# Moving the input projection's elementwise work from GpSimd to VectorE and ScalarE

## The chip, the cores and the metric

The kernel runs on one core of a Trainium2 chip. Its time is device time in microseconds of one execution, given as the median of several runs. The core has five instruction streams that run at once and wait for each other by semaphores: TensorE (PE, matrix multiplication into the accumulator memory PSUM), VectorE (DVE), ScalarE (ACT, functions and scaled copies), GpSimd (POOL, here used for elementwise operations) and SyncE (SP), which only issues DMA transfers. Each stream runs its instructions strictly in the order in which they were written out: an instruction that waits holds up everything behind it on the same engine.

## The reference

One layer of a bidirectional encoder, 1024 tokens of width 1024, float32. Cut to what the change touches, the first sub-layer is:

```
h = rms_norm(x); proj = h @ w_in
aq, ak, av, dqkv, dgate, dalpha, dbeta = split(proj)
aq, ak = rope(aq), rope(ak)                      # x1*cos - x2*sin, x2*cos + x1*sin
attn = window_attention(aq, ak, av, sink)        # +-128 tokens
q, k, v = silu(conv5(dqkv)); q, k = l2norm(q), l2norm(k)
g = -exp(a_log) * softplus(dalpha + dt_bias); beta = sigmoid(dbeta)
# gated delta rule in chunks, once forwards and once backwards:
decay[i, j] = exp(sum of g between j and i)
lower = strict_triangle((k*beta) @ k.T * decay); u, w = solve(I + lower, ...)
qk = (q @ k.T) * decay (triangle);  state recurrence over the chunks
mix = concat(attn, delta) @ w_out
```

Cross-attention and a feed-forward layer follow; the change does not touch them.

## The kernel before, in words

Matrix products that must keep float32 accuracy are made of three products in the reduced format F32R: each operand is split into a high part `hi` (a rounded copy, ScalarE, L102) and a low part `lo` (the difference, L103), and hi*hi, lo*hi and hi*lo are added in PSUM (`gemm_b`, L259). `load_w` loads a weight tile (`wraw`), splits it into `whi` and `wlo`, and takes the engine for the low part as an argument; there are two buffers of each.

The input projection has 22 column blocks of 128. For each of four heads the delta part takes three of them (`delta_proj`), convolves them (`conv`: two copies out of PSUM and a first tap on ScalarE, L281 and L282, then four taps on VectorE, L284, then Silu on ScalarE, L285) and prepares the chunk matrices (`prep`). `prep(h)` works on two halves of four chunks of 128 tokens, interleaved. For a half it builds `gm`, for each direction the triangle mask times the head's log decay `G` (L459, POOL), and multiplies it with a triangle in float32 on TensorE (L460); `E` is the exponential of the sum (L462). The products k*k (`U`) and q*k (`pc`) are multiplied by `E` on VectorE, and `pc` is masked twice into `pm` (L496, POOL), one for each direction, which are stored through DRAM for the later scan.

`base_inverse(g)` inverts the 32 x 32 diagonal blocks of two heads: thirty pairs of short VectorE operations (L536 `tmpb`, L538 `A`), each waiting for the one before. `levels(h)` builds the 128 x 128 inverse from them: block-diagonal tiles D5, D6, Z0 and Z1 are made by a mask (L579, half of them on POOL), with small matmuls (L595, L601) between. `attn_proj` applies the rotary embedding: VectorE makes `sn` (L737) and `rop` (L738), four DMAs move `sn`'s quarters to other partitions (`rot`, L742), and `rop + rot` is formed on POOL (L743) and stored. `window` is one block of window attention; `scan` is the recurrence, which begins when the levels are stored.

Python code lists the stages in the tables ORDER_1 (`D`: projection of a head, `P`: prep, `B`: base inverse), ORDER_2 (`L`: levels, `A`, `V`, `G`: attention, value and gate projections, `W`: two windows) and ORDER_3 (the scan). A scheduler then sets the order of each engine's instructions from priorities and its own estimates of their lengths, so a moved instruction also moves others.

Of the kernel before, what the change touches and what calls it, by code (L numbers as in the profile page):

```python
# [10 lines left out]
F32 = mybir.dt.float32  # L11
# [8 lines left out]
P = 128  # L20
# [3 lines left out]
NT = S // P  # L24
# [51 lines left out]
def tile_hybrid_block(  # L76
# [16 lines left out]
    def f32(ap):  # L93
        return ap.bitcast(F32)

    def bc(ap, axis, shape):
        return ap.unsqueeze(axis).to_broadcast(list(shape))
# [39 lines left out]
    sm = p12.enter_context(pool("sm", 1))  # L137
    C0, C1 = _AT["mUi"], _AT["mU"]
    C = sm.tile([P, C1 - C0], F32, name="C")
    mU_s = sm.tile([P, P], F32, name="mU_s")  # L140
    mL_s = sm.tile([P, P], F32, name="mL_s")
    prm = sm.tile([P, 24], F32, name="prm")
    nega = sm.tile([P, 8], F32, name="nega")
    p1 = ExitStack()
# [97 lines left out]
    nc.scalar.copy(cols, pt[:, :P])  # L242
    nc.sync.dma_start(CE, consts[:, C1:])
    nc.sync.dma_start(C, consts[:, C0:C1])
    nc.vector.tensor_copy(mU_s, cm["mU"])
    nc.vector.tensor_copy(mL_s, cm["mL"])

    nc.sync.dma_start(prm[:, 0:8], a_log[0].rearrange("d h -> (d h)").partition_broadcast(P))
    nc.sync.dma_start(prm[:, 8:16], dt_bias[0].rearrange("d h -> (d h)").partition_broadcast(P))
# [12 lines left out]
    def proj(src_cols, eng=None):  # L262
        whi, wlo = load_w(src_cols, KT, P, eng)
        pp = [pg.tile([P, 512], F32, tag="pg", name="pg") for _ in range(2)]
        gemm_b(whi, wlo, hT, pp)
        return pp
# [82 lines left out]
    dump("G", G)  # L349
    dump("beta", beta)  # L350


    pt = small()
    pv = pt[:, 0:192].rearrange("p (s d n) -> p s d n", s=3, d=2)
# [85 lines left out]
    def prep(h, kc, qc, vc):  # L440

        g, hh = h // 2, h % 2
        for src, i in ((kc, 2), (qc, 3)):
            nc.sync.dma_start(d_kv[g][:, :, hh, i].rearrange("c p n -> p c n"), src.rearrange("p (c n) -> p c n", c=NT))
        def part(b):
            c4 = slice(4 * b, 4 * b + 4)

            def turned(src):
                p_ = small()
                for j in range(4):  # L450
                    o = (4 * b + j) * P
                    nc.tensor.transpose(p_[:, j * P:(j + 1) * P], src[:, o:o + P], ident)
                return p_.rearrange("p (c n) -> p c n", c=4)


            pa = small()
            for d, (mi, ml) in enumerate((("mUi", mL_s), ("mLi", mU_s))):
                gm = t2.tile([P, 4, P], F32, tag="gm", name="gm")
                nc.gpsimd.tensor_tensor(gm, bc(G[:, d, h, c4], 2, (P, 4, P)), bc(cm[mi], 1, (P, 4, P)), ALU.mult)  # L459
                nc.tensor.matmul(pa, ml, gm.rearrange("p c n -> p (c n)"), start=(d == 0), stop=(d == 1))  # L460
            E = t2.tile([P, 4, P], F32, tag="E", name="E")
            nc.scalar.activation(E, pa.rearrange("p (c n) -> p c n", c=4), AF.Exp)  # L462

            def squares(pk, rev):
                ss = t2.tile([P, 4], F32, tag="ss4", name="ss4", bufs=4)
                for j in range(4):
                    jk = t2.tile([P, P], F32, tag="jk", name="jk")
                    o = 3 - j if rev else j
                    nc.scalar.activation(jk, pk[:, j, :], AF.Square, accum_out=ss[:, o:o + 1])
                return ss  # L470

            kv = t2.tile([P, 4, 2, P], F32, tag="kv", name="kv")
            yield
            pk = turned(kc)
            nc.scalar.copy(kv[:, :, 0, :], pk)
            ss = squares(pk, False)
            nc.gpsimd.tensor_scalar(xk[:, h, c4], ss, EPS, None, ALU.add)
            nc.gpsimd.tensor_tensor(rootk[:, h, c4], xk[:, h, c4], phalf[:, 0:4], ALU.pow)
            if hh and b:
                beta_rows(g)  # L480
            for i, src in ((2, kc), (3, qc)):
                yield
                p_ = small().rearrange("p (c n) -> p c n", c=4)
                for j in range(4):
                    o = (4 * b + j) * P
                    nc.tensor.matmul(p_[:, j, :], kc[:, o:o + P], src[:, o:o + P], start=True, stop=True)
                if i == 2:
                    U = t2.tile([P, 4, P], F32, tag="U", name="U")
                    nc.vector.tensor_tensor(U, p_, E, ALU.mult)
                    nc.sync.dma_start(d_u[g][hh, c4].rearrange("c p n -> p c n"), U)  # L490
                else:
                    pc = t2.tile([P, 4, P], F32, tag="pc", name="pc")
                    nc.vector.tensor_tensor(pc, p_, E, ALU.mult)
                    for d, mi in enumerate(("mUi", "mLi")):
                        pm = t2.tile([P, 4, P], F32, tag="pm", name="pm", bufs=3)
                        nc.gpsimd.tensor_tensor(pm, pc, bc(cm[mi], 1, (P, 4, P)), ALU.mult)  # L496
                        unsaved.append((d_pz[g][d][c4, :, hh, 0].rearrange("c p n -> p c n"), pm))
            yield

            nc.gpsimd.tensor_scalar(epsq[:, g, :, 1 - b, hh], squares(turned(qc), b == 0), P * EPS, P * EPS * EPS,  # L500
                                    ALU.mult, ALU.add)
            yield
            nc.vector.tensor_tensor(kv[:, :, 1, :], turned(vc), bc(rootk[:, h, c4], 2, (P, 4, P)), ALU.mult)
            nc.sync.dma_start(d_kv[g][c4, :, hh, 0:2].rearrange("c p s n -> p c s n"), kv)
            if h < 3:
                save()

        together([part(b) for b in range(2)])
# [39 lines left out]
    def levels(h):  # L548
# [21 lines left out]
        def part(b):  # L570
# [4 lines left out]

            L5, L6, D5, D6 = wide("L5"), wide("L6"), wide("D5"), wide("D6")
            Z = [wide("Z0"), wide("Z1")]
            for e, dst, src in ((nc.vector, D5, c5), (nc.gpsimd, D6, c6), (nc.vector, Z[0], cz[0]), (nc.gpsimd, Z[1], cz[1])):
                e.tensor_tensor(dst.rearrange("p c (q n) -> p c q n", q=4), bc(src[:, c4, :], 2, (P, 4, 4, 32)),  # L579
                                        bc(dmask, 1, (P, 4, 4, 32)), ALU.mult)  # L580
            Ul = wide("Ul")
# [126 lines left out]
    def delta_proj(h):  # L708
        kqv[h] = kqv.get(h, [])
        for i in (1, 0, 2)[len(kqv[h]):]:  # L710
            kqv[h].append(conv(proj(dcols(i, h), nc.gpsimd), 4 * i + h))


    def issue(order, table):
# [14 lines left out]
    def attn_proj(ct):  # L729
        pp = proj(w_in[:, ct * P:(ct + 1) * P])  # L730
        dst = d_q[ct * P:(ct + 1) * P, :] if ct < 4 else d_k
        for hf in range(2):
            sl = slice(hf * HALF, (hf + 1) * HALF)
            rop = trp.tile([P, HALF], F32, tag="rop", name="rop")
            sn = trp.tile([P, HALF], F32, tag="rot", name="sn")
            rot = trp.tile([P, HALF], F32, tag="rot2", name="rot2")
            nc.vector.tensor_tensor(sn, pp[hf], sinT[:, sl], ALU.mult)  # L737
            nc.vector.tensor_tensor(rop, pp[hf], cosT[:, sl], ALU.mult)  # L738

            for q in range(4):  # L740
                o = 32 * (q ^ 1)
                nc.sync.dma_start(rot[32 * q:32 * q + 32], sn[o:o + 32])  # L742
            nc.gpsimd.tensor_tensor(rop, rop, rot, ALU.add)  # L743
            nc.sync.dma_start(dst[:, sl], rop)

    def value_proj():
# [778 lines left out]
```

## Time and profile before

| what | value |
|---|---|
| median of 3 runs | 1586.01 us (1585.48 to 1587.09) |
| the profiled execution | 1581.95 us, its span 1580.1 us |
| busy, share of the span | PE 95%, DVE 66%, ACT 47%, POOL 29% |
| mean granted TensorE clock | 0.985 |

"Span" is the time from the first to the last instruction. The profile lists, for groups of equal instructions, the source line, the engine, the operation, output and inputs by name, their count, their busy time and mean duration, and the idle time of that engine just ahead of them with what ended it. PE's durations include a part in which the next matmul is already running, so their distance tells their cost better than their duration.

The input projection lasts until about 396 us, when the last level tiles are stored; the scan follows until about 555 us, and the output projection begins at 595 us. Everything that the change touches directly lies in the first 396 us.

### The profile page before, as it was taken

What the parts mean: (1) busy time and instruction counts of PE and PEld (TensorE: products, weight loads), DVE (VectorE), ACT (ScalarE), POOL (GpSimd) and SP (SyncE); (2) the same over time, 40 slices, a digit from 0 to 9 for tenths busy, and PEclk for the clock granted to TensorE, in tenths of its full rate; (3) what the DMA queues carried; (4) which work ended last, traced back from release to release, by engine and by line L of the source; (5) the groups of instructions that cost most, each with busy time, mean ns of one, the idle gap of its engine ahead of it and who ended that gap; (6) DMA issues with size and microseconds to landing.
All of it is one profiled execution on the core that took longest, in us unless ns stands there. A gap on an engine that the chain in (4) does not pass through costs nothing.

```text
span 1580.1 us, 21010 instructions
## 1 busy us (share of the span) xinstructions
PE 1503.9 (95%) x7451; PEld 1256.4 (80%) x7451; DVE 1047.9 (66%) x1609; ACT 748.8 (47%) x1504; POOL 462.1 (29%) x432
## 2 busy tenths in 40 slices
PE   6999898999899989999999999999999999999998
PEld 5777777778799867788888777788888888888786
DVE  6855977965688865444346448777768654586665
ACT  6564452246866764564335566332232332444532
POOL 2364433232234500253301140433434433100021
PEclk9999999999999999999999999999999999999999
DMA  6244337473998585454222264443335333853354
GB/s 208 67 129 120 107 107 180 134 187 111 318 293 276 164 271 184 157 187 147 74 73 94 67 206 139 125 150 121 127 110 164 100 101 106 294 202 112 107 171 162
DMA packets 260485, 242.95 MB, mean 154 GB/s; under 512 B 33672, under 2 KB 199453, under 8 KB 260381
## 3 DMA queue, kind: packets, MB, share of 16 engines
q1 hardware_dynamic: 260381, 241.62, 48.6%
q8 instruction: 58, 0.95, 0.2%
q14 instruction: 46, 0.38, 0.1%
HBM read 172.07 MB, written 66.88 MB: 151 GB/s over the span
## 4 chain that ended last, share of the span: by engine, by line
PE 74%; DVE 11%; DMA 6%; ACT 4%; issue 2%; SPq 1%; POOL 1%; DVEq 0%; POOLq 0%; ACTq 0%
PE pmg L1021 10%; PE pD L1196 7%; PE pE L1196 7%; PE pg L259 7%; PE pA L1196 6%; PE pcq L259 6%; PE pdX L1386 5%; PE pdA L1386 4%; PE pB L1196 4%; PE psc L790 3%; DVE acc L284 3%; PE pdD L1386 2%; PE pcs L1102 1%; PE pco L1128 1%; PE pck L921 1%
## 5 line engine op out<-in xcount | busy, mean ns | idle before, releaser
L102 ACT CAST whi<-wraw 128x1024 fp32r<-128x1024 f32 x108 | 113.1, 1049 | 149.7 <-DMA wraw<-in_w_gate_up_dram 30.9
L103 POOL TENSOR_TENSOR wlo<-wraw,whi 128x1024 fp32r<-128x1024 f32 x48 | 117.9, 2456 | 191.1 <-ACT whi L102 168.6
L259 PE MATMUL pg<-hhi,whi 128*128 128x512 f32 x352 | 141.0, 401 | 0.0
L259 PE MATMUL pg<-hhi,wlo 128*128 128x512 f32 x352 | 140.8, 400 | 0.0
L259 PE MATMUL pg<-hlo,whi 128*128 128x512 f32 x352 | 140.3, 399 | 0.0
L103 DVE TENSOR_TENSOR wlo<-wraw,whi 128x1024 fp32r<-128x1024 f32 x60 | 74.4, 1243 | 76.8 <-ACT whi L102 72.6
L1021 PE MATMUL pmg<-whi,b 128*128 128x512 f32 x384 | 118.4, 395 | 2.7 <-ACT whi L102 2.2
L1196 PE MATMUL pA<-s,whi 128*128 128x512 f32 x352 | 109.6, 392 | 1.4 <-ACT m L1213 1.4
L284 DVE SCALAR_TENSOR_TENSOR acc<-cp,cols,acc 128x1024 f32<-128x1024 f32 x48 | 77.2, 1610 | 19.2 <-ACT acc L282 14.0
L1021 PEld LDWEIGHTS pmg<-whi,b 128*128 128x128 f32 x384 | 71.2, 188 | 17.9 <-ACT whi L102 2.7
L259 PEld LDWEIGHTS pg<-hhi,whi 128*128 128x128 f32 x352 | 67.2, 191 | 14.4 <-issue 0.7
L259 PEld LDWEIGHTS pg<-hlo,whi 128*128 128x128 f32 x352 | 67.1, 191 | 14.2 <-issue 1.0
L259 PEld LDWEIGHTS pg<-hhi,wlo 128*128 128x128 f32 x352 | 67.4, 191 | 13.6 <-issue 0.5
L1386 PE MATMUL pdX<-dhl,whi 128*128 128x512 f32 x264 | 76.1, 390 | 1.5 <-DVE zv L1441 0.8
L1196 PEld LDWEIGHTS pA<-s,whi 128*128 128x128 f32 x352 | 65.3, 188 | 15.2 <-ACT m L1213 2.0
L1273 POOL TENSOR_TENSOR act<-act,up 128x512 f32<-128x512 f32 x33 | 50.1, 1519 | 88.0 <-DVE up L1272 53.2
L1021 PE MATMUL pmg<-wlo,b 128*128 128x512 f32 x192 | 71.4, 392 | 0.0
L1196 PE MATMUL pA<-s,wlo 128*128 128x512 f32 x176 | 68.7, 391 | 1.1 <-DVE wlo L103 1.1
L102 ACT CAST whi<-araw 128x1024 fp32r<-128x1024 f32 (+1 forms) x36 | 35.4, 982 | 71.5 <-PE pdX L1386 27.6
L1416 POOL TENSOR_SCALAR frs<-sq 128x1 f32<-128x1 f32 x8 | 11.9, 1497 | 195.5 <-ACT jk L1405 194.6
L1245 POOL TENSOR_TENSOR sr<-wraw 128x512 f32<-128x512 f32 x22 | 29.9, 1359 | 128.5 <-DMA wraw<-in_w_gate_up_dram 128.4
L103 DVE TENSOR_TENSOR wlo<-araw,whi 128x1024 fp32r<-128x1024 f32 (+1 forms) x36 | 40.8, 1133 | 39.5 <-ACT whi L102 39.4
(408 smaller groups left out, 4158.9 us busy)
## 6 DMA issues: line engine op xcount, KB each, us to landing
wraw<-in_w_gate_up_dram SPq DMA_DIRECT2D x52, 512.0 KB, 3.9
kv<-d_kv SPq DMA_DIRECT2D x32, 512.0 KB, 7.3
wraw<-in_w_in_dram SPq DMA_DIRECT2D x22, 512.0 KB, 4.7
b<-in_w_down_dram SPq DMA_DIRECT2D x20, 512.0 KB, 6.8
araw<-d_as SPq DMA_DIRECT2D x20, 512.0 KB, 3.7
pz<-d_pz SPq DMA_DIRECT2D x32, 256.0 KB, 7.1
wraw<-in_w_ckv_dram SPq DMA_DIRECT2D x16, 512.0 KB, 7.6
wraw<-in_w_out_dram SPq DMA_DIRECT2D x16, 512.0 KB, 4.1
```

The source lines that it names most:

```text
L102: nc.scalar.copy(hi, src)
L103: (eng or nc.vector).tensor_tensor(lo, src, f32(hi), ALU.subtract)
L259: nc.tensor.matmul(p_, w[:, k, :], ah[a][:, k, :], start=(k == 0 and i == 0), stop=(k == nk - 1 and i == 2))
L284: nc.vector.scalar_tensor_tensor(acc, cp[:, t:t + S], taps[t], acc, ALU.mult, ALU.add)
L790: nc.tensor.matmul(out[:, d, h, :], lt[:, d, h, :], rt[:, d, h, :], start=True, stop=True)
L921: nc.tensor.matmul(pp, w[:, k, :], mT[a][:, k, :], start=(k == 0 and i == 0), stop=(k == KT - 1 and i == 2))
L1021: nc.tensor.matmul(pp[t], act[a][:, k, tt], w_[:, kk, :], start=(k == 0 and i == 0), stop=(k == KT - 1 and i == 2))
L1102: nc.tensor.matmul(pp[:, t2_, :], q[a][:, ct, tt], kr_[b_][:, ct, :], start=(j == 0 and i == 0), stop=(j == 1 and i == 2))
L1196: nc.tensor.matmul(out_, w[a][:, k, :], xx[b_][:, k, :], start=(start and k == 0 and i == 0), stop=(k == HK - 1 and i == 2), skip_group_ch ...
L1245: nc.gpsimd.tensor_tensor(s[0], b_[:, 0:HK], b_[:, HK:], ALU.add)
L1273: nc.gpsimd.tensor_tensor(o_, o_, up, ALU.mult)
L1386: nc.tensor.matmul(banks[t], a[:, k - k0, tt], w, start=(first and k == 0 and i == 0), stop=(k == NB - 1 and i == 2), skip_group_check=not ...
```

## The change

Operations of the input projection move away from POOL:

- the masks `pm`, the level tiles D6 and Z1 and the rotary addition go to VectorE;
- the low parts of the delta projection's weights go to VectorE (`proj` without an engine);
- `gm` goes to ScalarE, as a scaled copy of the mask, one chunk at a time. Since it is now in F32R, `G` is first split into a high and a low part (`ghi`, `glo`), and each half has four `gm` tiles of four activations each and four F32R matmuls, in place of two tiles and two float32 matmuls. The triangles `mU_r` and `mL_r` are F32R too.

POOL keeps small operations (square roots, memsets), the base inverse's mask and scaling, and the windows' low parts.

```diff
-    mU_s = sm.tile([P, P], F32, name="mU_s")
-    mL_s = sm.tile([P, P], F32, name="mL_s")
+    mU_r = sm.tile([P, P], F32R, name="mU_r")
+    mL_r = sm.tile([P, P], F32R, name="mL_r")
...
-    nc.vector.tensor_copy(mU_s, cm["mU"])
-    nc.vector.tensor_copy(mL_s, cm["mL"])
+    nc.vector.tensor_copy(mU_r, cm["mU"])
+    nc.vector.tensor_copy(mL_r, cm["mL"])
...
+    ghi = sm.tile([P, 2, 4, NT], F32, name="ghi")
+    glo = sm.tile([P, 2, 4, NT], F32, name="glo")
+    ghr = t1.tile([P, 2, 4, NT], F32R, tag="ghr", name="ghr")
+    nc.vector.tensor_copy(ghr, G)
+    nc.vector.tensor_copy(ghi, f32(ghr))
+    nc.vector.tensor_tensor(glo, G, ghi, ALU.subtract)
...
             pa = small()
-            for d, (mi, ml) in enumerate((("mUi", mL_s), ("mLi", mU_s))):
-                gm = t2.tile([P, 4, P], F32, tag="gm", name="gm")
-                nc.gpsimd.tensor_tensor(gm, bc(G[:, d, h, c4], 2, (P, 4, P)), bc(cm[mi], 1, (P, 4, P)), ALU.mult)
-                nc.tensor.matmul(pa, ml, gm.rearrange("p c n -> p (c n)"), start=(d == 0), stop=(d == 1))
+            n = 0
+            for d, (mi, ml) in enumerate((("mUi", mL_r), ("mLi", mU_r))):
+                for part in (ghi, glo):
+                    gm = t2.tile([P, 4, P], F32R, tag="gm", name="gm")
+                    for j in range(4):
+                        nc.scalar.activation(gm[:, j, :], cm[mi], AF.Identity, scale=part[:, d, h, 4 * b + j:4 * b + j + 1])
+                    nc.tensor.matmul(pa, ml, gm.rearrange("p c n -> p (c n)"), start=(n == 0), stop=(n == 3))
+                    n += 1
...
-                        nc.gpsimd.tensor_tensor(pm, pc, bc(cm[mi], 1, (P, 4, P)), ALU.mult)
+                        nc.vector.tensor_tensor(pm, pc, bc(cm[mi], 1, (P, 4, P)), ALU.mult)
...
-            for e, dst, src in ((nc.vector, D5, c5), (nc.gpsimd, D6, c6), (nc.vector, Z[0], cz[0]), (nc.gpsimd, Z[1], cz[1])):
+            for e, dst, src in ((nc.vector, D5, c5), (nc.vector, D6, c6), (nc.vector, Z[0], cz[0]), (nc.vector, Z[1], cz[1])):
...
-            kqv[h].append(conv(proj(dcols(i, h), nc.gpsimd), 4 * i + h))
+            kqv[h].append(conv(proj(dcols(i, h)), 4 * i + h))
...
-            nc.gpsimd.tensor_tensor(rop, rop, rot, ALU.add)
+            nc.vector.tensor_tensor(rop, rop, rot, ALU.add)
```

The order of the instructions on three places follows. Lines of the changed kernel are up to ten higher than those of the kernel before (L462 becomes L472, L743 becomes L753).

ScalarE where the first head is prepared, before: `whi` is the weights' high part, `cp` and `acc` the convolution's inputs, `EG` other decays, `E` the decay matrix.

```order
L345 ACTIVATE xa<-ab 128x64
L102 CAST whi<-wraw 128x1024
L281 COPY cp<-pg 128x512
L282 ACTIVATE acc<-pg,cols 128x512
L361 ACTIVATE EG<-ps 128x3x32
L363 ACTIVATE EG<-ps 128x3x4 x8
L462 ACTIVATE E<-ps 128x512
L285 ACT_TABLE_LOAD
L285 ACTIVATE acc<-acc 128x1024
```

The same place of ScalarE in the changed kernel:

```order
L345 ACTIVATE xa<-ab 128x64
L468 ACTIVATE gm<-C,ghi 128x128 x4
L102 CAST whi<-wraw 128x1024
L281 COPY cp<-pg 128x512
L282 ACTIVATE acc<-pg,cols 128x512
L468 ACTIVATE gm<-C,glo 128x128 x4
L367 ACTIVATE EG<-ps 128x3x32
L369 ACTIVATE EG<-ps 128x3x4 x8
L468 ACTIVATE gm<-C,ghi 128x128 x4
L281 COPY cp<-pg 128x512
L282 ACTIVATE acc<-pg,cols 128x512
L468 ACTIVATE gm<-C,glo 128x128 x4
```

Four groups of `gm` stand between the copies, and the first `E` comes only behind the second half's first group and a Silu.

VectorE at the end of the first base inverse and at the head of the second, before (`kv` are the turned keys and values, `Z` and `D` level tiles):

```order
L540 TENSOR_TENSOR V<-A,bB 128x32x32
L103 TENSOR_TENSOR wlo<-wraw,whi 128x1024
L284 SCALAR_TENSOR_TENSOR acc<-cp,cols,acc 128x1024 x4
L432 RECIPROCAL xi_1811<-xk 128x16
L433 TENSOR_TENSOR bp_1810<-beta,xi_1811 128x32
L103 TENSOR_TENSOR wlo<-wraw,whi 128x1024
L489 TENSOR_TENSOR U<-ps,E 128x512 x2
L493 TENSOR_TENSOR pc<-ps,E 128x512 x2
L503 TENSOR_TENSOR kv<-ps,rootk 128x4x128 x2
L527 SCALAR_TENSOR_TENSOR A<-V,bB 64x1024
```

The same place of VectorE in the changed kernel:

```order
L550 TENSOR_TENSOR V<-A,bB 128x32x32
L438 RECIPROCAL xi_1961<-xk 128x16
L439 TENSOR_TENSOR bp_1960<-beta,xi_1961 128x32
L103 TENSOR_TENSOR wlo<-wraw,whi 128x1024
L499 TENSOR_TENSOR U<-ps,E 128x512 x2
L503 TENSOR_TENSOR pc<-ps,E 128x512
L506 TENSOR_TENSOR pm<-pc,C 128x512 x2
L503 TENSOR_TENSOR pc<-ps,E 128x512
L506 TENSOR_TENSOR pm<-pc,C 128x512
L513 TENSOR_TENSOR kv<-ps,rootk 128x4x128 x2
L747 TENSOR_TENSOR sn<-pg,sinT 128x512
L748 TENSOR_TENSOR rop<-pg,cosT 128x512
```

The last convolution (four rows L284) no longer stands behind the inverse: it was put inside it. Masks follow the products, and the first attention projection's rotary rows come ahead of the second inverse.

VectorE within the second base inverse, in the changed kernel: two rotary additions, which wait for the transfer `rot`, stand some rows behind the `sn` that the transfer moves.

```order
L753 TENSOR_TENSOR rop<-rop,rot_2845 128x512
L546 TENSOR_TENSOR tmpb<-A 128x234
L747 TENSOR_TENSOR sn<-pg,sinT 128x512
L748 TENSOR_TENSOR rop<-pg,cosT 128x512
L548 TENSOR_TENSOR A<-A,tmpb 128x18x13
L103 TENSOR_TENSOR wlo<-wraw,whi 128x1024
L546 TENSOR_TENSOR tmpb<-A 128x238
L548 TENSOR_TENSOR A<-A,tmpb 128x17x14
L546 TENSOR_TENSOR tmpb<-A 128x240
L548 TENSOR_TENSOR A<-A,tmpb 128x16x15
L753 TENSOR_TENSOR rop<-rop,rot_2856 128x512
```

In the kernel before no rotary addition stands on VectorE at all; its rows there are the inverse, `sn`, `rop` and low parts.

## The prediction

> **What bounds the kernel now.** The page's busy tenths come first, 40 slices of 39.5 us each. The input projection, with the delta preparation, the base inverses, the levels and the first windows, fills slices 1 to 10.
>
> ```profile
> PE   6999898999899989999999999999999999999998
> DVE  6855977965688865444346448777768654586665
> ```
>
> TensorE is nearly full everywhere; VectorE is full in slices 5 and 8, with seven tenths between them. The change is worth what TensorE loses there. The busy time by stretch, in windows that I chose at the two base inverses, shows it; the columns are the window, its length, busy time of PE, weight loads, DVE, ACT and POOL, then the granted clock.
>
> ```profile
> 40.00:153.00 113.00, 110.47 (x536) 89.17 (x535) 72.13 (x72) 64.17 (x148) 53.94 (x52) 1.00 0.37 106
> 153.00:222.00 69.00, 60.14 (x268) 46.83 (x267) 65.12 (x89) 30.87 (x66) 26.57 (x27) 0.95 0.41 118
> ...
> 246.00:321.00 75.00, 66.77 (x331) 56.45 (x331) 68.56 (x130) 20.09 (x47) 24.72 (x17) 0.91 0.64 154
> 321.00:396.00 75.00, 71.31 (x405) 61.35 (x403) 47.25 (x105) 42.71 (x105) 23.99 (x21) 0.98 0.55 149
> ```
>
> From 153 to 222 DVE is 94% busy and PE idle 8.9 us; from 246 to 321 DVE is 91% busy and PE idle 8.2 us. The clock takes more: 5% of 69 is 3.5 us, 9% of 75 is 6.7 us. With 2.5 us idle in the first row, and 3.7 idle and 1.5 of clock in the last, TensorE loses about 35 us between 40 and 396. That is the most that feeding it better can give.
>
> What POOL does to DVE is seen where both run (time, duration, engine, line):
>
> ```profile
> 163.00 2.35 POOL L103 TENSOR_TENSOR wlo<-wraw,whi 128x1024 fp32r<-128x1024 f32 x1 [0.91 <-ACT whi L102]
> ```
> ```profile
> 162.74 0.25 DVE L538 TENSOR_TENSOR A<-A,tmpb 128x84 f32<-128x84 f32 x1
> 163.02 2.46 DVE L536 TENSOR_TENSOR tmpb<-A 128x108 f32<-128x108 f32 x1
> ```
>
> A 108-element multiply, whose neighbour of 84 took 0.25 us, lasted 2.46 us, until the POOL operation ended. POOL's time is thus DVE's time wherever DVE has a two-input operation to run.
>
> **The change part by part.** First what DVE gains and gets, in groups from 40 to 396 us (busy us, mean ns):
>
> ```profile
> L284 DVE SCALAR_TENSOR_TENSOR acc<-cp,cols,acc 128x1024 f32<-128x1024 f32 x48 | 77.2, 1610 | 19.2 <-ACT acc L282 14.0 <-POOL gm L459 4.4
> L536 DVE TENSOR_TENSOR tmpb<-A 128x30 f32<-128x30 f32 (+14 forms) x60 | 32.0, 533 | 1.3
> L538 DVE TENSOR_TENSOR A<-A,tmpb 128x30 f32<-128x30 f32 (+14 forms) x60 | 24.3, 406 | 1.6
> L103 DVE TENSOR_TENSOR wlo<-wraw,whi 128x1024 fp32r<-128x1024 f32 x10 | 13.2, 1319 | 0.5 <-ACT whi L102 0.4
> L579 DVE TENSOR_TENSOR Z<-cz,dmask 128x512 f32<-128x512 f32 x8 | 9.1, 1152 | 2.3 <-DMA d_pz<-Z 2.3
> ...
> L579 DVE TENSOR_TENSOR D<-c,dmask 128x512 f32<-128x512 f32 x8 | 5.3, 686 | 2.3 <-PE ps L601 2.3
> ```
> ```profile
> L284 DVE SCALAR_TENSOR_TENSOR acc<-cp,cols,acc x48: 1273/1284/3414, 46.1 to 220.7; 128x1024 f32<-128x1024 f32 x48
> ```
> ```profile
> L103 POOL TENSOR_TENSOR wlo<-wraw,whi 128x1024 fp32r<-128x1024 f32 x10 | 25.3, 2532 | 18.6 <-DVE ang L378 13.5 <-ACT whi L102 4.9
> L496 POOL TENSOR_TENSOR pm<-pc,C 128x512 f32<-128x512 f32 x16 | 23.9, 1512 | 21.3 <-DVE pc L493 11.7 <-DMA d_pz<-pm 9.4
> L459 POOL TENSOR_TENSOR gm<-G,C 128x512 f32<-128x512 f32 x16 | 21.3, 1338 | 11.2 <-DVE G L344 7.0 <-PE ps L460 4.1
> L743 POOL TENSOR_TENSOR rop<-rop,rot 128x512 f32<-128x512 f32 x10 | 13.7, 1372 | 44.3 <-DMA rot<-sn 33.5 <-DVE tmpb L536 7.0 <-DMA qr<-d_q 3.8
> L579 POOL TENSOR_TENSOR Z<-cz,dmask 128x512 f32<-128x512 f32 x8 | 10.9, 1371 | 13.6 <-DMA d_pz<-Z 5.9 <-DVE rop L738 4.4 <-DVE Z L579 2.7
> L579 POOL TENSOR_TENSOR D<-c,dmask 128x512 f32<-128x512 f32 x8 | 10.4, 1310 | 13.8 <-PE ps L601 13.8
> ```
>
> POOL loses 25.3 + 23.9 + 21.3 + 13.7 + 10.9 + 10.4 = 105.5 us. DVE loses blocked time: the convolution 48 x (1.610 - 1.273) = 16.2; the inverse rows 56.3 against some 38.8 if each shape took its shortest copy (0.19 to 0.40 us), so 17.5; Z 9.1 - 8 x 0.686 = 3.6; about 37 in all. DVE gets ten low parts at 1.32 (13.2) and 42 operations of the size of D at 0.686 (16 masks, 16 level tiles, 10 rotary additions: 28.8), plus three small ones for glo at about 0.2: 42.6 us. At the blocked Z's 1.152 instead, the 42 would cost 48.4. **VectorE's total hardly moves;** what counts is where.
>
> From 153 to 222:
>
> ```profile
> L284 DVE SCALAR_TENSOR_TENSOR acc<-cp,cols,acc 128x1024 f32<-128x1024 f32 x18 | 27.1, 1505 | 0.2
> L536 DVE TENSOR_TENSOR tmpb<-A 128x30 f32<-128x30 f32 (+14 forms) x30 | 17.0, 568 | 0.7
> L538 DVE TENSOR_TENSOR A<-A,tmpb 128x30 f32<-128x30 f32 (+14 forms) x30 | 12.4, 414 | 0.7
> ```
> ```profile
> 217.61 2.08 PE L460 MATMUL ps<-gm,mL_s 128*128 128x512 f32 x2 [3.74 <-POOL gm L459]
> ```
>
> Blocked time here is 27.1 - 18 x 1.273 = 4.2 plus 29.4 - 19.4 = 10.0; added are three low parts more (4.0) and four masks (2.7): a net relief of 7.5 us. The 3.74 us wait for gm goes as well, since ScalarE makes it and need not queue behind POOL's scaling of A (L541). By the new order the last convolution of head 3 stands inside the inverse, not behind it. I take -8 of the 12.4 that PE loses here; the ends are 0 and -12.
>
> Two more operations wait at the head of VectorE's queue instead of POOL's. A low part waits for the cast of whi; behind it stand convolutions, which wait for copies that ScalarE makes after that cast, so I take 0 and keep POOL's own 4.9 us of such waits (first POOL row) as the end. The fourth mask of a head waits until the first is stored (three buffers): POOL waited 9.4 us once for it (second POOL row), when the base inverse's loads stood ahead on the SP queue; the new order puts that mask behind the inverse's first row, which waits for those loads anyway: 0, with 5 as the end.
>
> From 246 to 321 the rest of the inverse's blocked time (7.5) and most of Z's and the low part's (4) go, and eight level tiles (5.5), some seven rotary additions (4.8) and one mask (0.7) come: even. But a rotary addition now waits for its transfer at the head of VectorE's queue:
>
> ```profile
> 294.08 0.68 DVE L738 TENSOR_TENSOR rop<-pg,cosT 128x512 f32<-128x512 f32 x1
> ```
> ```profile
> 294.19 2.45 SPq L742 DMA_DIRECT2D rot<-sn  x4
> ```
> ```profile
> DMA to landing us min/median/max: 1.9/2.0/6.1
> ```
>
> From the end of sn (294.1) the four issues and the landing need 2.45 + 2.0 = 4.5 us. The new order leaves 8 to 20 rows between, worth 3.4 us (a low part and six short rows) to over 10. Five of the ten are close; at 0 to 1 us each I take +3. The ends are 0 and the second rival's price. In 321 to 396 DVE is 63% busy and hides its eight level tiles and three additions; without that cover they would cost 7.5.
>
> **The masked decay.** Two fp32 matmuls of 512 columns start 0.86 us apart, the F32R ones 22.47 / 99 = 0.227 us:
>
> ```profile
> 206.05 1.02 PE L460 MATMUL ps<-gm,mL_s 128*128 128x512 f32 x2
> 206.91 1.02 PE L460 MATMUL ps<-gm,mU_s 128*128 128x512 f32 x2
> ```
> ```profile
> 89.15 22.47 PE pg L259 x99
> ```
>
> 16 x 0.86 = 13.8 us become 32 x 0.227 = 7.3: **-6.5 us** of TensorE, on its path, since by the four windows it is busy 308.7 of 332 us. ScalarE gets 128 activations of 128 elements. No such row exists; the nearest are
>
> ```profile
> L469 ACT ACTIVATE jk<-ps 128x128 f32<-128x128 f32 x64 | 17.0, 295 | 9.0 <-PE ps L452 9.0
> L469 ACT ACTIVATION_READ_ACCUMULATOR jk<-ps 128x1 f32 x64 | 14.4, 226 | 0.0
> L282 ACT ACTIVATE acc<-pg,cols 128x512 f32<-128x512 f32 x22 | 15.4, 701 | 0.0
> ```
>
> from 0.175 (a quarter of L282) to 0.49 (jk with its read), 22 to 63 us; jk and its read overlap to a pitch of 0.25, which I take: 32 us, a group of four 1.0. ScalarE is busy 95 of 182 us from 40 to 222, so that covers it; without cover every group would be paid. What is queued behind it matters: the cast of whi, the copies out of PSUM, Silu, and E. E of each of the eight half heads now has one group and one matmul more ahead of it. Most of that is filled by projection matmuls put between; I take +2, ends 0 and 8 x 1.25 = +10.
>
> The Trainium skill's page "ScalarE: Activation LUTs" speaks against this edit. Its section "What ACT_TABLE_LOAD costs" gives an ACTIVATE 186 ns plus 0.833 per element and 93 per pointer operand, less 93 of overlap back to back: by it a gm activation is an estimated 0.293 us, all of them 37.5, and the sum would be about 0.4 us worse (2 x 37.5 / 32). Its "Rules for kernel authors" put multiplications on VectorE rather than ScalarE; the busy rows above have VectorE full at that place and ScalarE half idle.
>
> **Behind the projection.** The scan's order is the same but for windows: some 15 TensorE rows move behind its start, +1.5 us. Otherwise it moves with its start at 1:1, ends +-4 for another meeting of transfers.
>
> **Sum.** -6.5 - 8 + 3 + 2 + 1.5 = -8, and I add -2 of clock (a quarter of the 8.2 us that it takes from 246 to 396): -10. The profiled execution took 1581.95 (span 1580.1), so 1572; the median of the runs, 1586.01, stands 4.06 above it, so **1576**.
>
> **The rivals.**
> 1. TensorE recovers most of its 35 us, since it need only stay fed. For it: the long waits of PE are few.
>
> ```profile
> PE ps L595 <- DVE L L588: 6.2, 2, 3.9
> PE ps L460 <- POOL gm L459: 4.9, 2, 3.7
> ```
>
> Against: DVE stays about 90% full in both stretches. With half of 35 and the 6.5: 1586 - 24 = 1562.
> The Trainium skill, "TensorE: Matmul & The Clock Gate", "What's actually happening", says that the clock falls to half after an idle window of about 3.4 us. By that rule, waits of 3.7 and 3.9 us cut a little shorter would return the clock whole; the trace agrees so far that the clock is 0.91 and 0.95 where those waits are. It would make this rival likelier, not change its price.
> 2. The rotary additions block VectorE. Where the SP queue is late, they wait much longer than 1 us:
>
> ```profile
> 316.82 0.68 DVE L737 TENSOR_TENSOR sn<-pg,sinT 128x512 f32<-128x512 f32 x1
> ```
> ```profile
> 327.12 1.29 POOL L743 TENSOR_TENSOR rop<-rop,rot 128x512 f32<-128x512 f32 x1 [7.80 <-DMA rot<-sn]
> ```
>
> That is 9.6 us from the end of sn. POOL waited 33.5 us for rot over eight additions; if DVE waits half of that, 17, in place of my 3, the sum is +4: 1590; with all of it, 1606. It decides from 13 us of such waits, 1.6 each. Against it: the new order has four of the ten over 10 us apart.
> 3. ScalarE is late and TensorE waits in order for gm, since only two gm tiles exist: at the +10 end in place of +2 and DVE's relief unused, 1586 - 6.5 + 3 + 10 + 1.5 = 1594.
> 4. It doesn't do what it says: the relief is refilled at once and only TensorE's 6.5 stands against the +6.5 of the other terms: 1586.
>
> **How the numbers follow.** Forecast (1570 to 1582) 0.45; rival 1 0.2; rival 4 0.15; rival 2 0.13; rival 3 0.07. The range from 1560 to 1592 leaves out half of rivals 1, 2 and 3, which is 0.2. A difference under 0.2%, about 3 us, can't be told from none. Faster 0.65, same 0.15, slower 0.2. The forecast's own range is 1570 to 1582.
>
> **What would show it.** POOL busy near 357 us; L284 near 1.28 us each and no inverse row over 0.5; 32 decay matmuls 0.23 us apart; gm activations near 0.25 us apart; the start of the scan (first psc, near 400) about 10 us earlier. Wrong if VectorE's waits ahead of the rotary additions exceed 13 us, if PE waits for gm more than 5 us, or if what is won by the scan's start is lost before the output projection (595).

## The result, and the profile after

| | median us | runs, lowest to highest | ratio to before, 95% interval |
|---|---|---|---|
| before | 1585.74 | 1585.41 to 1587.09 | |
| the changed kernel | 1566.15 | 1563.36 to 1570.83 | 0.9878 [0.9849, 0.9907] |

The change takes 19.6 us off, about twice the 10 that was forecast; 1566.15 lies below the forecast's own range of 1570 to 1582. The profiled executions stand 18.1 us apart by their spans (1580.1 and 1562.0), and that is the difference to be found.

The busy time by engine before, then the page of the changed kernel with the busy tenths of TensorE and VectorE.

```profile
PE 1503.9 (95%) x7451; PEld 1256.4 (80%) x7451; DVE 1047.9 (66%) x1609; ACT 748.8 (47%) x1504; POOL 462.1 (29%) x432
```
```profile
PE 1501.4 (96%) x7451; PEld 1260.0 (81%) x7451; DVE 1041.5 (67%) x1664; ACT 787.0 (50%) x1632; POOL 357.4 (23%) x364
...
PE   6999999988999999999999999999999999999997
...
DVE  6765878966789765444355457776867654696665
```

POOL has lost 104.7 us (462.1 before). VectorE's total is 6.4 us less (1047.9 before), although it runs 55 instructions more. TensorE no longer falls to 8 tenths in slices 5 and 7, but does in slices 9 and 10.

VectorE's groups in the changed kernel from 40 to 385 us (busy us, mean ns, then the idle time just ahead and what ended it):

```profile
L284 DVE SCALAR_TENSOR_TENSOR acc<-cp,cols,acc 128x1024 f32<-128x1024 f32 x48 | 62.5, 1303 | 0.7
L103 DVE TENSOR_TENSOR wlo<-wraw,whi 128x1024 fp32r<-128x1024 f32 x20 | 24.4, 1221 | 21.6 <-ACT whi L102 21.6
L548 DVE TENSOR_TENSOR A<-A,tmpb 128x30 f32<-128x30 f32 (+14 forms) x60 | 19.8, 330 | 1.4
L546 DVE TENSOR_TENSOR tmpb<-A 128x30 f32<-128x30 f32 (+14 forms) x60 | 19.7, 329 | 1.3
L589 DVE TENSOR_TENSOR D<-c,dmask 128x512 f32<-128x512 f32 x16 | 10.7, 689 | 2.6 <-PE ps L611 2.3
L506 DVE TENSOR_TENSOR pm<-pc,C 128x512 f32<-128x512 f32 x16 | 10.5, 688 | 3.3 <-DMA d_pz<-pm 3.2
L589 DVE TENSOR_TENSOR Z<-cz,dmask 128x512 f32<-128x512 f32 x16 | 10.5, 686 | 3.9 <-DMA d_pz<-Z 3.9
...
L753 DVE TENSOR_TENSOR rop<-rop,rot 128x512 f32<-128x512 f32 x10 | 7.9, 786 | 5.6 <-DMA rot<-sn 3.9 <-issue 1.7
```

The convolution's taps are down from 1610 to 1303 ns, the inverse's rows from 533 and 406 to 329 and 330: 14.7 + 16.8 = 31.5 us are gone, and neither group's mean shows blocking any more (one rotary addition, L753, still took 1.67 us). The waits moved: the convolution's 19.2 us became 0.7, and the low parts, now ahead in the same queue, wait 21.6 us for ScalarE's casts.

For TensorE the clearest cut is the start of the scan, the first `psc`. Its row before and after (durations, then first and last start):

```profile
L790 PE MATMUL psc<-kv,pz x128: 270/275/377, 405.6 to 540.0; 128*128 128x128 f32 x128
```
```profile
L800 PE MATMUL psc<-kv,pz x128: 270/275/445, 389.8 to 525.9; 128*128 128x128 f32 x128
```

Windows that I set from 40 us to that point, before and after (length, busy time of PE, weight loads, DVE, ACT, POOL, clock):

```profile
40.00:405.60 365.60, 339.01 (x1690) 278.76 (x1689) 264.82 (x419) 180.66 (x430) 139.44 (x132) 0.96 0.48 131
```
```profile
40.00:389.80 349.80, 331.61 (x1679) 278.86 (x1677) 257.66 (x469) 215.97 (x553) 34.16 (x64) 0.96 0.49 136
```

The scan starts 15.8 us earlier: TensorE is busy 7.4 us less and idle 8.4 us less (18.2 after 26.6). The granted clock is 0.96 in both: by the traces' clock records half the clock was granted for 27.3 us of the first window and for 30.7 us of the second. The 7.4 us are the masked decay: counted by the busy time that each matmul adds, its matmuls take 15.4 us before and 7.9 after, all others 323.3 and 323.4.

What ended TensorE's idle time up to the scan is the second half of it. Of the kernel before, the prediction shows the two largest waits (6.2 us for L, 4.9 for gm); the next two, and then the three largest of the changed kernel, are (us in total, times, longest):

```profile
PE ps L486 <- DVE U L489: 3.6, 1, 3.6
PE ps L586 <- DVE Z L618: 3.1, 1, 3.1
```
```profile
PE ps L469 <- ACT gm L468: 3.7, 1, 3.7
PE ps L605 <- ACT m L576: 2.6, 1, 2.6
PE ps L605 <- DVE mov L623: 2.5, 3, 1.7
```

Added up by the engine that ended them, as the profile names it, all such waits fall from 16.7 to 7.3 us for VectorE and from 4.9 to 0 for POOL, and rise from 3.1 to 8.7 for ScalarE; 2 us are for transfers in both. So 14.3 us of waits went and 5.6 came. Of the remaining 2.3 us, 3.9 are won up to the output projection (first `pmg` at 595.9 and 576.2) and 1.6 are lost behind it.

By stretch, before and after, in equal windows:

```profile
163.00:218.00 55.00, 46.14 (x215) 37.04 (x214) 52.35 (x77) 28.80 (x64) 22.63 (x23) 0.96 0.42 121
239.00:300.00 61.00, 54.66 (x268) 45.49 (x266) 52.53 (x95) 14.93 (x33) 19.40 (x13) 0.94 0.63 157
300.00:385.00 85.00, 79.43 (x430) 68.35 (x431) 58.48 (x128) 41.92 (x106) 29.31 (x25) 0.94 0.61 160
```
```profile
163.00:218.00 55.00, 51.26 (x248) 42.77 (x247) 50.56 (x90) 40.78 (x110) 6.78 (x12) 0.94 0.40 121
239.00:300.00 61.00, 58.41 (x314) 49.16 (x313) 55.98 (x119) 15.84 (x39) 1.77 (x1) 1.00 0.66 171
300.00:385.00 85.00, 75.87 (x383) 64.51 (x381) 60.09 (x142) 46.66 (x113) 9.64 (x11) 0.86 0.55 144
```

TensorE issues 33 and 46 matmuls more beside the two inverses, with VectorE about as busy as it was, and so has fewer left for the last stretch, where it now idles 9.1 us at a clock of 0.86. Of these 9.1 us, waits in the levels' chains are 5.4 and waits in the window attention 3.6.

### The profile page after: what moved, and what is told of

Read it like the earlier page. It is cut to its first block, busy times and chain, and to the rows that moved or that the text cites. A ratio compares the mean times of both kernels' runs of the same rounds, so it can differ in the third digit from the quotient of the medians.

```text
span 1562.0 us, 21077 instructions
## 1 busy us (share of the span) xinstructions
PE 1501.4 (96%) x7451; PEld 1260.0 (81%) x7451; DVE 1041.5 (67%) x1664; ACT 787.0 (50%) x1632; POOL 357.4 (23%) x364
## 4 chain that ended last, share of the span: by engine, by line
PE 65%; DMA 4%; ACT 3%; DVE 3%; issue 2%; POOL 1%; SPq 0%; DVEq 0%; POOLq 0%; ACTq 0%
PE pmg L1031 9%; PE pD L1206 8%; PE pE L1206 8%; PE pA L1206 6%; PE pcq L259 6%; PE pdX L1396 6%; PE pdA L1396 4%; PE pB L1206 4%; PE psc L800 3%; PE pdD L1396 2%; PE pcs L1112 1%; PE pck L931 1%; PE pco L1138 1%; PE pdX L1489 1%; DMA kv<-d_kv 1%
## 5 line engine op out<-in xcount | busy, mean ns | idle before, releaser
L103 DVE TENSOR_TENSOR wlo<-wraw,whi 128x1024 fp32r<-128x1024 f32 x70 | 85.7, 1226 | 98.1 <-ACT whi L102 93.8
L103 POOL TENSOR_TENSOR wlo<-wraw,whi 128x1024 fp32r<-128x1024 f32 x38 | 92.9, 2444 | 164.7 <-ACT whi L102 163.6
L1031 PEld LDWEIGHTS pmg<-whi,b 128*128 128x128 f32 x384 | 72.0, 190 | 18.1 <-ACT whi L102 2.7
L284 DVE SCALAR_TENSOR_TENSOR acc<-cp,cols,acc 128x1024 f32<-128x1024 f32 x48 | 62.5, 1303 | 0.7
L1396 PEld LDWEIGHTS pdX<-dhl,whi 128*128 128x128 f32 x264 | 49.3, 188 | 12.8 <-issue 1.1
```

Of the source, the lines that this page charges most:

```text
L103: (eng or nc.vector).tensor_tensor(lo, src, f32(hi), ALU.subtract)
L284: nc.vector.scalar_tensor_tensor(acc, cp[:, t:t + S], taps[t], acc, ALU.mult, ALU.add)
L1031: nc.tensor.matmul(pp[t], act[a][:, k, tt], w_[:, kk, :], start=(k == 0 and i == 0), stop=(k == KT - 1 and i == 2))
L1396: nc.tensor.matmul(banks[t], a[:, k - k0, tt], w, start=(first and k == 0 and i == 0), stop=(k == NB - 1 and i == 2), skip_group_check=not ...
```

## The experiments

Each kernel was timed in three rounds beside the kernel before, whose median in the three sessions was 1585.73 (the first four kernels), 1587.44 (the next four) and 1586.18 (the last four). The table gathers them; columns 2 to 5 are from the one profiled execution of each kernel (those of act_fp32 and after_tail took 5.5 and 7.1 us more than their medians).

| kernel | first psc, us | PE busy, 40 to psc | PE idle, 40 to psc | psc to pmg | median us | ratio, interval |
|---|---|---|---|---|---|---|
| before | 405.6 | 339.0 | 26.6 | 190.3 | 1585.74 | |
| changed | 389.8 | 331.6 | 18.2 | 186.4 | 1566.15 | 0.9878 [0.9849, 0.9907] |
| only_gm | 409.2 | 336.9 | 32.3 | 188.6 | 1587.87 | 1.0003 [0.9991, 1.0015] |
| only_dve | 399.6 | 336.6 | 23.0 | 190.9 | 1581.79 | 0.9975 [0.9964, 0.9987] |
| act_fp32 | 402.3 | 340.1 | 22.2 | 191.0 | 1577.38 | 0.9946 [0.9930, 0.9963] |
| dummy_tt | 399.4 | 334.4 | 25.0 | 190.9 | 1578.80 | 0.9956 [0.9940, 0.9971] |
| dummy_memset | 392.7 | 332.6 | 20.1 | 185.6 | 1569.22 | 0.9887 [0.9872, 0.9901] |
| pe_more | 394.3 | 338.3 | 16.0 | 186.7 | 1567.40 | 0.9881 [0.9857, 0.9905] |
| before_o600 | 405.8 | 339.3 | 26.5 | 188.0 | 1588.57 | 1.0012 [1.0003, 1.0022] |
| before_tail | 407.1 | 338.6 | 28.5 | 183.9 | 1584.54 | 0.9985 [0.9972, 0.9999] |
| after_o60 | 392.3 | 328.6 | 23.7 | 192.5 | 1576.36 | 0.9931 [0.9916, 0.9946] |
| after_tail | 389.5 | 329.8 | 19.7 | 200.7 | 1571.88 | 0.9913 [0.9879, 0.9946] |
| act_fp32_tail | 399.2 | 338.4 | 20.8 | 188.9 | 1575.34 | 0.9930 [0.9907, 0.9954] |
| after_fewer | 391.1 | 334.7 | 16.4 | 194.4 | 1576.74 | 0.9934 [0.9909, 0.9958] |

### One half of the change at a time

only_gm keeps the new decay (ScalarE, F32R) and gives POOL its four other kinds of operation back:

```diff
-                        nc.vector.tensor_tensor(pm, pc, bc(cm[mi], 1, (P, 4, P)), ALU.mult)
+                        nc.gpsimd.tensor_tensor(pm, pc, bc(cm[mi], 1, (P, 4, P)), ALU.mult)
...
-            kqv[h].append(conv(proj(dcols(i, h)), 4 * i + h))
+            kqv[h].append(conv(proj(dcols(i, h), nc.gpsimd), 4 * i + h))
...
-            nc.vector.tensor_tensor(rop, rop, rot, ALU.add)
+            nc.gpsimd.tensor_tensor(rop, rop, rot, ALU.add)
```

(and D6 and Z1 likewise). Expected:

> The changed kernel with the masks, level tiles, low parts and rotary additions back on GpSimd: only the masked decay is changed (ScalarE, F32R). Relief theory (GpSimd's blocking of VectorE is most of the gain): only 21 of 105 us leave GpSimd, so TensorE's 6.5 us and little more is won, 1577 to 1581. Matmul theory (the gain is TensorE's work and gm's earlier arrival): most of the 19.6 us is here, 1566 to 1571. Order theory (another order of the same work made the difference): anything from 1560 to 1590, with VectorE's blocked time as before.

only_dve is the reverse: the four moves to VectorE made in the kernel before, gm left on POOL in float32. Expected:

> The kernel before with the masks, level tiles, low parts and rotary additions on VectorE, but the masked decay still on GpSimd in float32. Relief theory: 84 of 105 us leave GpSimd, 1571 to 1576, L284 near 1.35 us. Matmul theory: 1580 to 1586. Order theory: anywhere.

The first gives nothing, the second 0.25%, both together 1.2%; both times lie above what the relief theory gave (1577 to 1581 and 1571 to 1576). In only_gm VectorE stays blocked, and its taps wait for ScalarE's copies (14.0 us of such waits before):

```profile
L284 DVE SCALAR_TENSOR_TENSOR acc<-cp,cols,acc 128x1024 f32<-128x1024 f32 x48 | 73.1, 1526 | 35.0 <-ACT acc L282 34.2
```

TensorE saves 2.1 us of busy time up to the scan and idles 5.7 us more; the idle time that ScalarE ended is 11.9 us, after 3.1. In only_dve POOL still makes gm, VectorE's taps take 1375 ns, and the scan starts 6.0 us earlier:

```profile
L284 DVE SCALAR_TENSOR_TENSOR acc<-cp,cols,acc 128x1024 f32<-128x1024 f32 x48 | 65.9, 1375 | 0.8
```

The terms of the sum were added as if independent, and their gains do not add up here (each kernel was also ordered anew).

act_fp32 takes the last step apart: all five moves off POOL, but gm and the decay matmuls stay in float32, 64 activations and 16 matmuls.

```diff
-                for part in (ghi, glo):
-                    gm = t2.tile([P, 4, P], F32R, tag="gm", name="gm")
...
+                gm = t2.tile([P, 4, P], F32, tag="gm", name="gm")
+                for j in range(4):
+                    nc.scalar.activation(gm[:, j, :], cm[mi], AF.Identity, scale=G[:, d, h, 4 * b + j:4 * b + j + 1])
+                nc.tensor.matmul(pa, ml, gm.rearrange("p c n -> p (c n)"), start=(d == 0), stop=(d == 1))
```

> The four moves, and gm on ScalarE but with two float32 tiles and matmuls per half instead of four F32R ones (half the activations). If TensorE's 6.5 us are on its path: 1570 to 1574. If ScalarE's 128 activations cost time: at or below 1566. If neither matters: 1566 within 3.

VectorE's relief is complete (L284 at 1303 ns, as in the changed kernel), yet only 8.4 of the 19.6 us are there, less than any of the three forecasts. Up to the scan TensorE is busy 8.5 us and idle 4.0 us more than in the changed kernel. Counted as above, 6.4 of the 8.5 are the decay's matmuls (14.4 against 7.9 us); the other 2 are work that merely stands ahead of the scan, 20 matmul records more (a float32 matmul leaves two records, so the decay has 32 in both kernels).

### What on POOL costs, and what does not

dummy_tt adds 32 products on POOL to the changed kernel, whose results nobody uses; every other instruction, on every engine, stands in the same order in the two traces. It is the cleanest pair of the study.

```diff
+            for _ in range(2):
+                dj = t2.tile([P, 4, P], F32, tag="dj", name="dj", bufs=1)
+                nc.gpsimd.tensor_tensor(dj, E, bc(cm["mUi"], 1, (P, 4, P)), ALU.mult)
...
                         nc.vector.tensor_tensor(pm, pc, bc(cm[mi], 1, (P, 4, P)), ALU.mult)
+                        dj = t2.tile([P, 4, P], F32, tag="dj", name="dj", bufs=1)
+                        nc.gpsimd.tensor_tensor(dj, pc, bc(cm[mi], 1, (P, 4, P)), ALU.mult)
```

> The changed kernel with 32 more GpSimd products of 512 columns (two of E, two of pc in each half head) whose results nobody reads; every other engine's order is the same. Relief theory: about 40 us of GpSimd time blocks VectorE again, at the old rate (37 blocked for 105) some 14 us of blocked VectorE time, L284's mean from 1.30 back over 1.4, and 4 to 12 us of the time: 1570 to 1578. Matmul and order theories: no change, 1566 within 3.

dummy_memset puts at the same places a POOL memset of the same 512 columns and a read of two:

```diff
+                nc.gpsimd.tensor_scalar(dj[:, 0, 0:2], E[:, 0, 0:2], 1.0, None, ALU.mult)
+                nc.gpsimd.memset(dj, 0.0)
```

> The same 32 places as dummy_tt, but GpSimd writes the 512 columns (a memset) and reads only two columns of E or pc first. Every other engine's order is again that of the changed kernel. If what blocks VectorE is a GpSimd operation that reads SBUF: VectorE's groups and the time stay those of the changed kernel, 1563 to 1570. If GpSimd's being busy at all blocks VectorE, or holds up its own small operations (the square roots): most of dummy_tt's 12.7 us again, 1572 to 1579.

The groups of dummy_tt from 40 to 385 us:

```profile
L284 DVE SCALAR_TENSOR_TENSOR acc<-cp,cols,acc 128x1024 f32<-128x1024 f32 x48 | 65.8, 1373 | 0.7
...
L511 POOL TENSOR_TENSOR dj<-pc,C 128x512 f32<-128x512 f32 x16 | 25.3, 1579 | 8.1 <-DVE pc L506 7.1
L475 POOL TENSOR_TENSOR dj<-E,C 128x512 f32<-128x512 f32 x16 | 24.5, 1530 | 37.6 <-ACT E L472 37.1
...
L551 DVE TENSOR_TENSOR tmpb<-A 128x30 f32<-128x30 f32 (+14 forms) x60 | 23.0, 384 | 1.3
```

And of dummy_memset:

```profile
L284 DVE SCALAR_TENSOR_TENSOR acc<-cp,cols,acc 128x1024 f32<-128x1024 f32 x48 | 62.5, 1304 | 0.7
...
L476 POOL MEMSET dj<- 128x512 f32 x16 | 8.4, 527 | 0.9
L513 POOL MEMSET dj<- 128x512 f32 x16 | 8.4, 527 | 0.9
...
L475 POOL TENSOR_SCALAR dj<-E 128x2 f32<-128x2 f32 x16 | 6.4, 398 | 36.3 <-ACT E L472 35.6
```

The products put 12.7 us on the time (ratios 0.0078 +- 0.0033 apart), 9.6 of them by the start of the scan; VectorE's busy time up to there is 274.35 - 257.66 = 16.7 us higher with not one instruction more:

```profile
40.00:399.40 359.40, 334.36 (x1674) 279.50 (x1673) 274.35 (x469) 215.19 (x553) 87.67 (x96) 0.95 0.49 133
```

Part of the delay reaches TensorE through ScalarE, whose Silu waits for the taps. These waits are 49.8 us before (27.3 + 22.5), 10.2 in the changed kernel and 25.4 in dummy_tt, the last two by these lines:

```profile
ACT acc L285 <- DVE acc L284: 5.8, 3, 4.4
ACT L285 <- DVE acc L284: 4.4, 2, 2.8
```
```profile
ACT acc L285 <- DVE acc L284: 14.6, 5, 5.5
ACT L285 <- DVE acc L284: 10.8, 2, 9.1
```

TensorE's waits for gm rise from 3.7 to 6.7 us. That the products hold E or pc longer is not the reason: the trace names no instruction that waits for one of them. The memsets put on 3.1 us by the medians and 0.0009 +- 0.0032 by the ratios, which can't be told from nothing, and VectorE's taps stay at 1304 ns. VectorE's busy time up to the scan is 257.4 us there, although POOL is busy 32.4 us more than in the changed kernel (53.5 more in dummy_tt). So VectorE's loss does not come from POOL's being busy or from its semaphores but from its large products, while VectorE has two-input work. The timelines of POOL and of VectorE in dummy_tt show one case:

```profile
171.62 2.24 POOL L475 TENSOR_TENSOR dj<-E,C 128x512 f32<-128x512 f32 x1
```
```profile
172.63 1.28 DVE L551 TENSOR_TENSOR tmpb<-A 128x30 f32<-128x30 f32 x1
```

A row that takes 0.19 us at its shortest ends at 173.91, just as the product does (173.86). The Trainium skill, "SBUF — State Buffer", "Who interferes with whom", says that a VectorE instruction with two SBUF inputs contends with a GpSimd instruction that reads SBUF and not with one that only writes it; the two kernels agree. The memsets are also shorter (0.53 against 1.5 us), which no run here separates from their not reading.

### TensorE's work

pe_more issues one F32R decay matmul of each half five times, each restarting the sum, 32 more in all (the scheduler also moves other rows):

```diff
-                    nc.tensor.matmul(pa, ml, gm.rearrange("p c n -> p (c n)"), start=(n == 0), stop=(n == 3))
+                    for r in range(5 if n == 0 else 1):
+                        nc.tensor.matmul(pa, ml, gm.rearrange("p c n -> p (c n)"), start=(n == 0), stop=(n == 3 or (n == 0 and r < 4)))
```

> The changed kernel with four more F32R matmuls in each half head (the first decay matmul is issued five times, each overwriting the one before): 32 x 0.227 = 7.3 us more for TensorE, nothing more for ScalarE or VectorE. If TensorE's work is on the path 1:1, as the 6.5 us of the prediction's sum: 1571 to 1575. If it is off the path: within 3 of 1566. If the lost 11 us of act_fp32 came from more than the work: over 1575 only by an order effect.

Its timeline has five of them in a row, which with 0.39 us for the last are 0.25 us apart, 8 us in all:

```profile
71.71 1.40 PE L470 MATMUL ps<-gm,mL_r 128*128 128x512 f32 x5
```

Up to the scan TensorE is busy 6.7 us longer and idle 2.2 us less, and the scan starts 4.5 us later. That would be rather more than half of the extra work, but it rests on one execution of each kernel, with rows moved, where order alone shifts that point by 1.5 to 2.8 us. The end time (0.0003 +- 0.0038 by the ratios, about 0.5 +- 6 us) can't tell 0 from 4.5.

### The same work in another order

A moved instruction moves others, so part of any difference may be the order alone. Two kernels change only the scheduler's constant AHEAD, from 300 to 600 in before_o600 and to 60 in after_o60.

> The kernel before with AHEAD = 600 in place of 300: the same instructions, in another order (some 990 rows of TensorE's moved). Order theory: more than 5 us away from 1585.7 either way. Relief and matmul theories: within 4.

> The changed kernel with AHEAD = 60: the same instructions, in another order (some 1500 rows of TensorE's moved). Order theory: the 19.6 us are partly the luck of one order, and this one comes out above 1572. Relief and matmul theories: within 5 of 1566.

Three more change only ORDER_2, in the kernel before, in the changed one and in act_fp32:

```diff
-ORDER_2 = "L0 L1 G0 G1 A4 V A0 A1 L2 L3 W W W A2 A3 G2 G3 W".split()
+ORDER_2 = "L0 L1 G0 G1 A4 V A0 A1 L2 L3 A2 A3 W W W G2 G3 W".split()
```

> The kernel before in the same other order of the tail, as a control. Theory A: a change of order moves it too, by 2 to 10 us to either side of 1586. If the whole gain were order, this would come to within 5 us of the changed kernel (1571 or less); by the relief theory it stays above 1576, since VectorE remains blocked as often.

> The changed kernel with the third and fourth rotary projections listed ahead of three of the window pairs instead of behind them; the work is the same. Theory A (VectorE's relief makes the gain, but how much of it reaches the scan depends on how the last levels and the windows are interleaved before it): the time moves by several us without any change of work, 1560 to 1578, and the move arises between 300 us and the first psc. Theory B (the gain is fixed by the amounts of work on the engines, order hardly counts): 1564 to 1568.

> The kernel with the four moves to VectorE and gm on ScalarE, but with float32 decay matmuls, in the same other order of the tail. It stood 11 us behind the changed kernel. Theory A (that gap was order): its distance from the changed kernel in the same order differs by over 4 us from 11, and may close or change its sign. Theory B (the gap is what the float32 matmuls cost): it stays 8 to 14 us behind the changed kernel in the same order.

The kernel before takes 1584.5 to 1588.6 in its three orders, the changed one 1566.2, 1571.9 and 1576.4. The gain is there in any pair, from 8 to 22 us, and for the changed kernel the order that was timed is the best of the three. I had expected an order to act ahead of the scan, and that was wrong: the start of the scan lies between 405.6 and 407.1 in one family and between 389.5 and 392.3 in the other. It is the stretch from the scan to the output projection that scatters, from 183.9 to 200.7 us, and in these six executions the changed kernel has the longer ones: 186.4, 192.5 and 200.7 against 190.3, 188.0 and 183.9. In after_tail, whose profiled execution took 1578.97, the projection begins at 590.2, hardly ahead of before_tail's 591.0. In its 200.7 us the granted clock is 0.92 (0.97 in the changed kernel), and the same 1246 matmuls keep TensorE busy 184.3 us in place of 176.7.

act_fp32_tail answers half of its question. Its end time stands 3.5 us behind after_tail instead of 11. By the ratios that is 2.7 +- 6.5 after 10.8 +- 5.3, so whether the gap closed is not shown. By the start of the scan it is still 9.7 us behind (12.5 in the first order), so that part shows in both orders; TensorE is 8.6 us busier up to there.

### Further in the same direction

after_fewer takes two more reading operations from POOL to VectorE: the scaling of A and the windows' low parts of qs.

```diff
-        nc.gpsimd.tensor_tensor(A, A, bc(bB, 2, (P, 32, 32)), ALU.mult)
+        nc.vector.tensor_tensor(A, A, bc(bB, 2, (P, 32, 32)), ALU.mult)
...
-        nc.gpsimd.tensor_tensor(qs[64:128], qr[64:128], f32(qs[64:128]), ALU.subtract)
+        nc.vector.tensor_tensor(qs[64:128], qr[64:128], f32(qs[64:128]), ALU.subtract)
```

> The changed kernel with two more kinds of reading operations moved from GpSimd to VectorE: the scaling at the end of each base inverse (2 x 1.9 us) and the windows' low parts of qs (16 x 1.27 us, half of them before the scan). Relief theory: at the rate of the unused products (12.7 us for 49.8 us of them, 0.25 each) 24 us less give -6, and VectorE gets 16 x 0.69 + 2 x 1.3 = 13.6 us, about a third of it beside other work's waits: 1562 to 1567. If VectorE's added time counts in full instead: 1570 to 1576.

It missed both forecasts: 1576.74, 8.9 +- 6 us behind the changed kernel by the ratios. The scan starts at 391.1, within the spread of the orders; the loss lies in the 194.4 us behind it, where 10 of the 16 qs operations are, but where order alone makes the changed kernel 6 and 14 us longer. Which of the two it is stays open. No version beat the changed kernel.

## Why the prediction was right, and where its size was off

**Right: faster, and by which mechanism.** VectorE was slowed by POOL's products, and TensorE waited for VectorE, directly and through ScalarE. dummy_tt shows it by putting such products back without moving anything else.

**The signs named beforehand.** POOL is busy 357.4 us (357 was named). L284 has 1303 ns (1280), the decay's matmuls are 0.25 us apart where pe_more has five in a row (0.23), and no inverse row takes over 0.41 us (0.5). The scan starts 15.8 us earlier (10). Rotary additions idle VectorE 5.6 us (13 was the limit), 3.9 of them for the transfer, and TensorE waits 3.7 us for gm (5 was the limit). The gain is still there at the output projection in the order that was timed. The gm activations are 0.29 us apart, not 0.25: in ScalarE's timeline of the changed kernel a group of four starts 1.17 us behind the one before it.

```profile
85.08 1.27 ACT L468 ACTIVATE gm<-C,glo 128x128 fp32r<-128x128 f32 x4
86.25 1.27 ACT L468 ACTIVATE gm<-C,ghi 128x128 fp32r<-128x128 f32 x4
```

That is the estimate that the prediction took from the Trainium skill, "ScalarE: Activation LUTs", "What ACT_TABLE_LOAD costs" (0.293); ScalarE was 62% busy from 40 us to the scan, and no run separates what the difference cost.

**The decay's -6.5 held: -7.5 was measured**, all of the 7.4 us of busy time that TensorE saves up to the scan.

**The step that failed is the size of the relief, -8.** It was taken for the stretch from 153 to 222 alone, and the second inverse was called even. There TensorE's idle time fell by 5.1 us only, from 8.9 to 3.8, but from 40 to 153 it fell by 2.5 and from 246 to 321, called even, by 5.3 (8.2 to 2.9). The same three windows of the prediction in the changed kernel:

```profile
40.00:153.00 113.00, 113.00 (x565) 94.64 (x564) 72.17 (x93) 91.06 (x228) 8.13 (x28) 1.00 0.32 94
153.00:222.00 69.00, 65.25 (x310) 54.36 (x309) 56.49 (x95) 52.08 (x142) 10.08 (x16) 0.95 0.49 143
246.00:321.00 75.00, 72.06 (x391) 60.47 (x390) 64.92 (x145) 20.74 (x49) 2.08 (x2) 1.00 0.63 166
```

Over the whole projection the waits that VectorE and POOL ended fell by 14.3 us. That the net, -8.4, is so near to -8 is luck: 5.6 us of new waits for ScalarE stand against the 14.3, and behind 300 us, where idle time and clock losses together are 10 us higher, work had been done earlier.

**The other terms.** For a late E +2 was charged: TensorE waits 0.8 us for E before and not at all after. ScalarE's charge came elsewhere and was larger: 3.7 us for gm, although the prediction had its 3.74 us wait for gm go, and 2.6 for the levels' m. The rotary additions, +3, wait 3.9 us for the transfer on VectorE; none of TensorE's waits is named after them, and what of them lies in the waits for VectorE was not isolated. The -2 of clock did not come: half the clock was granted for 27.3 us before and for 30.7 after. From the scan to the output projection 3.9 us were won, where +1.5 was charged, but that stretch varies by 17 us between orders, so neither sign is shown. The low parts' wait for whi, taken at 0 with 4.9 as its end, came to 21.6 us; it stands where the convolution's waits of 19.2 stood, for the same engine, and what it cost net was not isolated.

**An argument that is not shown:** "on its path, since by the four windows it is busy 308.7 of 332 us". In only_gm the same cheaper matmuls (8.5 us in place of 15.4) bring nothing. Its TensorE idles 11.9 us until ScalarE is done, after 3.1, and its other matmuls are busy 4.9 us longer, so the 6.9 us are made up for elsewhere. A high busy share did not show where the saving would go.

**The rivals.** The first, 1562, is nearer in time than my 1576, but not by its mechanism: it had TensorE recover half of its 35 us and the clock return. Of 26.6 us idle up to the scan 8.4 came back, and the clock stayed at 0.96: it rose to 1.00 in the second inverse and fell to 0.86 behind it. The Trainium skill, "TensorE: Matmul & The Clock Gate", "What's actually happening", has the clock fall to half after an idle window of about 3.4 us. The second inverse agrees: its wait of 3.9 us is gone, and the clock with it is whole. Behind 300 us the longest wait is 2.6 us, and yet half the clock was granted for 23.9 us, each time behind a stretch of 3.4 us in which TensorE was still 27 to 56% busy; shorter waits were not enough there. Rotary waits (rival 2) stayed under their price. Rival 3, a late ScalarE, shows most in only_gm, as taps that wait 34.2 us for its copies; in the changed kernel it is the 5.6 us of TensorE's waits above. Rival 4, no gain at all, is near what the halves alone gave, not the whole.

**Not settled:** some 5 us of the 19.6. The mean over three orders is 1571.5 for the changed kernel and 1586.3 for the one before, 14.8 apart; what the timed order adds arises behind the scan's start, and why that stretch is 184 us long in one order and 201 in another was traced no further than the clock in after_tail.

## What to carry to other kernels

Count part of the time of GpSimd's large SBUF-reading operations as VectorE's wherever VectorE runs two-input work (here 49.8 us of them cost VectorE 16.7), and take all of them out of such a stretch before judging the idea: the halves here gave 0 and 4 us, the whole 20. Terms of a sum that rest on two engines taking turns as the limit need not add up, and a high busy share alone does not put a saving on the path; the waits, added up by the engine that ended them, say more. Compare two or three orders of the same work at an early milestone (here the start of the scan, within 3 us) before reading a cause into the last 10 us of the end time.

## What was not expected of the hardware

A POOL memset of 128x512 takes 0.53 us, the same on all 32, and leaves VectorE's two-input taps at 1304 ns, where 32 products of that shape raise them to 1373. The products themselves vary with what VectorE runs: in dummy_tt the two that meet no two-input row of VectorE take 1.27 us each, and others up to 2.34, so each engine waits for the other.
